# Two weight blocks and one left operand of a down projection loaded on another queue, one of the blocks into its own place

## The chip, the cores and the metric

The kernel runs on one core of a Trainium2 chip. The metric is the device time of one execution in microseconds (us); lower is better. The time before is 1745.2 us, the median of 3 runs (1744.49 to 1745.47). The names of the engines are those of the profile: PE multiplies matrices (PEld are its weight loads), DVE, ACT and POOL work on vectors, and SP issues DMAs. POOL issues DMAs as well, on a queue of its own.

## The reference

One decoder block on 1024 tokens of width 1024, all float32: three gated attention branches, an output projection with a residual, and an MLP. Only the MLP's last line is touched by the change:

```python
h2 = rmsnorm(x, g_mlp_norm[l])
u = jax.nn.relu(jnp.einsum('bsd,df->bsf', h2, w_ff_up[l]))
x = x + jnp.einsum('bsf,fd->bsd', u * u, w_ff_down[l])
```

`w_ff_down` has 4096 rows and 1024 columns. The output is `x`, 1024 by 1024.

## The kernel before

Each float32 operand of a matrix product is split into a rounded part (hi, made by ACT) and the rest (lo, made by DVE as operand minus hi), and a product takes three passes on PE: hi by hi, hi by lo, lo by hi. The large projections are done by a scheme of Strassen's kind: instead of eight block products of a two by two block multiplication there are seven, named P1 to P7, on sums and differences of blocks.

**The up projection** ends in `evict_ops`. Its results, squared and already combined into the seven left operands of the next projection, are stored to a scratch tensor in memory, `s_scr`, by POOL's queue (line 1690), 128 rows of 512 numbers (256 KB) each.

**The down projection** (from `V = Pool("v", ...)` on) runs through `plan`: four groups j of the inner dimension, and in each group the seven products of `DOWN`, in the order P1, P2, P6, P7, P5, P4, P3. Step k of `plan` is one product of one group: four output tiles t, each with 4 blocks by 3 passes, so 48 matmuls of 128x512 (line 2343). While step k runs on PE, the operands of step k+1 are made: `right` makes the weight operand (the sum of blocks on DVE in `right_sum`, then hi on ACT at line 2261, then lo on DVE), `left` makes hi (line 2272) and lo of the left operand. Every two-input operation on DVE goes through the helper `tt`, so all of them carry line 1609.

The weight blocks of a group are w11, w12, w21 and w22, 128 x 2048 numbers (1 MB) each, loaded by `load_wb` (line 2225). They live in four places g0 to g3 of the pool RA by the table `side_of`: w21 in g0, w12 in g1, w22 in g2, w11 in g3. In the first group of the kernel before, w11 is an exception: it goes into the place "t1" of the pool V, and t1 = w12 - w11 is formed in place. The pool V takes over memory that the up projection's tiles have held. The places g0 to g3 hold the operands of P1 and P2 of the up projection until the last such product is done; "g2" and "g3" are those of P2.

The left operands are loaded by `load_s` (line 2233) into three buffers "ur", 1 MB each. The first step's operands are made earlier (`first_load`, `first_split`, line 2162 and after).

Steps in the first group that matter here: k=0 is P1 (operands ready before), k=1 is P2 (w21 as it is, and s of P2), k=2 is P6 (t1 = w12 - w11 and then t2 = w22 - t1, and s of P6), k=3 is P7 (t3 = w22 - w12). In the trace t1 and t2 both read as `t`, the weight operands as `h` (for k=1: `sop`), the hi and lo of the left operands as `sop`, the blocks as `g`, the loaded left operands as `ur`.

The order of work on every engine is the order in which the program is written; nothing reorders it. SP and POOL each issue their DMAs in that order too, and an issue that waits for its place holds everything behind it on the same queue.

Of the kernel before, what the change touches and what calls it, by code (L numbers as in the profile page):

```python
# [21 lines left out]
P = 128  # L22
# [21 lines left out]
def tile_hybrid_block(  # L44
# [20 lines left out]
    nc = tc.nc  # L65
# [58 lines left out]
    s_scr = dram.tile([7 * DFF // 2, S // 2], F32, name="s_scr", tag="s_scr")  # L124
# [1483 lines left out]
    def tt(out_, a_, b_, op):  # L1608
        nc.vector.tensor_tensor(out_, a_, b_, op)  # L1609
# [125 lines left out]
    with tc.manual_schedule():  # L1735
# [79 lines left out]
        rows = [], []  # L1815
# [393 lines left out]
        def vt(tag, dt=F32):  # L2209
            if tag in side_of:  # L2210
                return RA.t(side_of[tag], [P, 4, 512], dt)
            return laid.pop(tag) if tag in laid else V.t(tag, [P, 4, 512], dt)
# [3 lines left out]
        plan = [(j, kind) for j in range(len(groups)) for kind in DOWN]  # L2216
        wb, sraw, sop, top = {}, {}, {}, {}

        def load_wb(j, tag, to=None):
            if j < len(groups):  # L2220
                p, n_ = groups[j]
                wb[j, tag] = vt(to or tag)[:, :n_]
                rows = w_down[2 * p * P:2 * (p + n_) * P, :].rearrange("(c i p) n -> i p c n", i=2, p=P)
                dh = int(tag[2]) - 1
                nc.sync.dma_start(wb[j, tag], rows[int(tag[1]) - 1][:, :, dh * 512:(dh + 1) * 512])

        def load_s(k):
            if k < len(plan):
                j, kind = plan[k]
                p, n_ = groups[j]  # L2230
                sraw[k] = vt("ur")[:, :n_]
                r0 = (DOWN.index(kind) * NP + p) * P
                nc.sync.dma_start(sraw[k], s_scr[r0:r0 + n_ * P, :].rearrange("(c p) n -> p c n", p=P))

        def right_sum(k):

            j, kind = plan[k]
            n_ = groups[j][1]
            if kind == "P6":
                r = wb[j, "t2"] = vt("t2")[:, :n_]  # L2240
                tt(r, wb[j, "w22"], wb[j, "t1"], ALU.subtract)
            elif kind == "P7":
                r = wb[j, "t3"] = vt("t3")[:, :n_]
                tt(r, wb[j, "w22"], wb[j, "w12"], ALU.subtract)
                load_wb(j + 1, "w12")
            elif kind == "P4":
                r = wb[j, "t4"] = vt("t4")[:, :n_]
                tt(r, wb[j, "w21"], wb[j, "t2"], ALU.subtract)
                load_wb(j + 1, "w21")
            else:  # L2250
                r = wb[j, {"P1": "w11", "P2": "w21", "P5": "t1", "P3": "w22"}[kind]]
            return r

        def right(k, part):
            j, kind = plan[k]
            n_ = groups[j][1]
            if part == 0:
                raw = right_sum(k)
                h_, l_ = operand(RA) if k > 1 else (vt("sop", F32R), vt("sop", F32R))
                top[k] = h_[:, :n_], l_[:, :n_], raw  # L2260
                nc.scalar.activation(top[k][0], raw, AF.Copy)  # L2261
            else:
                h_, l_, raw = top[k]
                tt(l_, raw, f32(h_), ALU.subtract)
                if kind == "P3":
                    load_wb(j + 1, "w22")

        def left(k, part):
            n_ = groups[plan[k][0]][1]
            if part == 0:  # L2270
                sop[k] = vt("sop", F32R)[:, :n_], vt("sop", F32R)[:, :n_]
                nc.scalar.activation(sop[k][0], sraw[k], AF.Copy)
            else:
                tt(sop[k][1], sraw[k], f32(sop[k][0]), ALU.subtract)

        sop[0], top[0] = pieces["u"], pieces["w"]
        load_wb(0, "w21")
        for k in (1, 2):
            load_s(k)
        load_wb(0, "w12")  # L2280
        load_wb(0, "w11", "t1")
        load_wb(0, "w22")


        Q = Pool("q", q=2)
# [2 lines left out]
        def late(n):  # L2288
            def rows(kind):
                r0 = (DOWN.index(kind) * NP + place(0)) * P  # L2290
                return s_scr[r0:r0 + P, :]

            def fetch_(key, src):
                q[key] = Q.t("q", [P, 512])
                nc.sync.dma_start(q[key], src)

            def made(kind, key, a_, b_, op):
                tt(q[key], q[a_], q[b_], op)
                keep(kind, 0, q[key])
            if n == 0:  # L2300
                fetch_("a21", u_scr[:, :])
                fetch_("a22", rows("P4"))
            elif n == 1:
                made("P5", "a22", "a21", "a22", ALU.add)
            elif n == 2:
                fetch_("a11", rows("P1"))
            elif n == 3:
                made("P7", "a21", "a11", "a21", ALU.subtract)
            elif n == 4:
                fetch_("s1", rows("P5"))  # L2310
            elif n == 5:
                made("P6", "s1", "s1", "a11", ALU.subtract)
            elif n == 6:
                fetch_("a12", rows("P2"))
            elif n == 7:
                made("P3", "a12", "a12", "s1", ALU.subtract)
# [4 lines left out]
        def out_evict(k, t):  # L2321
            j, kind = plan[k]
            ps = (bx if kind in ("P1", "P6", "P5", "P3") else by)[t]
            s = t if kind in ("P1", "P2", "P3") else 4 + t
            dh = kind in ("P7", "P5", "P3")
            a_ = xr[s][:, dh * 512:(dh + 1) * 512]
            if j == 0 and kind in ("P1", "P6", "P7", "P3"):
                nc.scalar.activation(a_, ps, AF.Copy)
            else:
                tt(a_, a_, ps, ALU.add)  # L2330
            if j == len(groups) - 1 and kind in ("P2", "P5", "P4", "P3"):
                nc.sync.dma_start(out[s * P:(s + 1) * P, dh * 512:(dh + 1) * 512], a_)

        x2t = {}
        for k, (j, kind) in enumerate(plan):
            n_ = groups[j][1]
            for t in range(4):
                ps = (bx if kind in ("P1", "P6", "P5", "P3") else by)[t]
                (sh, sl), (th, tl) = sop[k], top[k][:2]
                qs = slice(t * P, (t + 1) * P)  # L2340
                for c in range(n_):
                    for i, (a_, b_) in enumerate(((sh, th), (sh, tl), (sl, th))):
                        nc.tensor.matmul(ps, a_[:, c, qs], b_[:, c, :],  # L2343
                                         start=(kind in ("P1", "P2", "P7") and c == 0 and i == 0),
                                         stop=(kind in ("P2", "P4", "P3") and c == n_ - 1 and i == 2),
                                         skip_group_check=True)
                if t or k:
                    out_evict(*((k, t - 1) if t else (k - 1, 3)))
                if t == 0 and k:
                    load_s(k + 2)  # L2350
                if k + 1 < len(plan):
                    if t == 0:
                        right(k + 1, 0)
                    elif t == 1:
                        right(k + 1, 1)
                        left(k + 1, 0)
                    elif t == 2:
                        left(k + 1, 1)
                if t == 3 and kind == "P1":
                    wb[j, "t1"] = vt("t1")[:, :n_] if j else wb[j, "w11"]  # L2360
                    tt(wb[j, "t1"], wb[j, "w12"], wb[j, "w11"], ALU.subtract)
                    load_wb(j + 1, "w11")
                if t == 0 and k in (8, 11, 15, 18):
                    x2t[k] = vt("ur").rearrange("p (s c) n -> p s (c n)", s=2)
                    s0 = 2 * (8, 11, 15, 18).index(k)
                    nc.sync.dma_start(x2t[k], x2_scr[s0 * P:(s0 + 2) * P, :].rearrange("(s p) n -> p s n", p=P))
                if t == 3 and k - 1 in x2t:
                    s0 = 2 * (8, 11, 15, 18).index(k - 1)
                    for i in range(2):
                        tt(xr[s0 + i], xr[s0 + i], x2t[k - 1][:, i, :], ALU.add)  # L2370
                if t == 3 and k >= 2:
                    late(k - 2)
# [31 lines left out]
```

## Time and profile before

| | |
|---|---|
| median of 3 runs | 1745.2 us |
| lowest and highest | 1744.49 and 1745.47 us |
| time of the profiled execution | 1743.94 us |
| its span | 1742.2 us |
| first matmul of the down projection | 1421.5 us after the span's start |
| memory read, written | 142.64 MB, 57.15 MB |

The profile is of one execution. The span is the time from the first to the last instruction that the profile shows; the execution's own time is 1.74 us longer. Times in rows of the trace count from the span's start. A row of the timeline gives the start, the duration, the engine, the line, the operation, output and inputs with their shapes, how many instructions of the kind are merged, and in brackets the idle time before and what ended it. The granted TensorE clock is full throughout.

### The profile page before, as it was taken

Reading aid. Unit: us, or ns where it says so; the run is one execution under the profiler, and the core shown is the slowest. Engines: PE = TensorE matmul, PEld = TensorE weight load, DVE = VectorE, ACT = ScalarE, POOL = GpSimd, SP = SyncE. Lnnn points to the kernel's source line nnn. Section 1 sums busy time; section 2 is a strip of 40 time slices with the busy share of each in tenths; the row PEclk is TensorE's granted clock in tenths of the full one; section 3 lists DMA queues with packets and bytes.
Section 4 is the critical chain, followed back from the end, with each engine's and each line's share of the span. In section 5 each row is a group of like instructions: output and inputs, shape, how many; then the busy total and the mean of one; then the engine's idle time right before and its main releaser. Section 6 shows DMA issues by size and latency. Waiting matters only on the chain.

```text
span 1742.2 us, 24834 instructions
## 1 busy us (share of the span) xinstructions
PE 1726.7 (99%) x9426; PEld 1475.3 (85%) x9426; DVE 1262.0 (72%) x2014; ACT 884.8 (51%) x1553; POOL 115.1 (7%) x298
## 2 busy tenths in 40 slices
PE   9999999999999999999999999999999999999999
PEld 9889989888988899899888887878888877888887
DVE  7524578677777567666887699887777776687875
ACT  6525575555566478767974336533332344333331
POOL 0101100000000000010000000121112110000000
PEclk9999999999999999999999999999999999999999
DMA  5241121122132311212354643144344475455531
GB/s 206 73 125 51 50 87 38 42 68 58 36 87 58 90 54 32 78 54 60 117 173 138 225 163 116 43 159 155 133 152 151 145 271 212 156 201 180 194 121 73
DMA packets 136328, 201.41 MB, mean 116 GB/s; under 512 B 9680, under 2 KB 73168, under 8 KB 136208
## 3 DMA queue, kind: packets, MB, share of 16 engines
q1 hardware_dynamic: 127168, 170.20, 30.3%
q0 software_dynamic: 9040, 29.63, 4.9%
q8 instruction: 74, 1.21, 0.3%
q14 instruction: 46, 0.38, 0.1%
HBM read 142.64 MB, written 57.15 MB: 115 GB/s over the span
## 4 chain that ended last, share of the span: by engine, by line
PE 84%; issue 6%; DVE 4%; ACT 2%; POOL 2%; DMA 1%; SPq 0%; POOLq 0%; DVEq 0%; ACTq 0%
PE pp L1040 37%; PE pp L2343 7%; PE pp L1673 6%; PE pv L894 4%; PE tr L2343 4%; PE sc L2343 4%; PE tr L874 4%; PE sc L1673 3%; PE pv L2343 2%; POOL s_scr L1690 1%; PE tr L1673 1%; PE sc L772 1%; PE sc L773 1%; PE tr L1916 1%; PE sc L815 1%
## 5 line engine op out<-in xcount | busy, mean ns | idle before, releaser
L1040 PE MATMUL pp<-hi,whi 128*128 128x512 f32 x496 | 199.1, 401 | 0.0
L1040 PE MATMUL pp<-hi,wlo 128*128 128x512 f32 x496 | 195.8, 395 | 0.0
L1040 PE MATMUL pp<-lo,whi 128*128 128x512 f32 x496 | 195.1, 393 | 0.0
L1040 PE MATMUL pp<-whi,hi 128*128 128x256 f32 (+1 forms) x640 | 183.3, 286 | 0.0
L1040 PE MATMUL pp<-whi,lo 128*128 128x256 f32 (+1 forms) x640 | 179.8, 281 | 0.2 <-DVE lo L487 0.2
L1040 PE MATMUL pp<-wlo,hi 128*128 128x256 f32 (+1 forms) x640 | 179.2, 280 | 0.0
L2343 PE MATMUL pp<-h,sop 128*128 128x512 f32 x540 | 129.0, 395 | 2.3 <-DVE sop L1609 2.3
L881 DVE TENSOR_TENSOR ptl<-tr,pth 128x512 fp32r<-128x512 f32 (+1 forms) x160 | 99.3, 632 | 43.2 <-ACT pth L879 42.3
L2343 PEld LDWEIGHTS pp<-h,sop 128*128 128x128 f32 x540 | 101.1, 187 | 27.7 <-DVE sop L1609 2.6
L879 ACT ACTIVATE pth<-tr 128x512 fp32r<-128x512 f32 (+1 forms) x160 | 86.3, 555 | 70.1 <-PE tr L874 41.8
L1673 PE MATMUL pp<-h,oh 128*128 128x512 f32 x384 | 120.9, 396 | 0.7 <-ACT cu L1759 0.6
L1040 PEld LDWEIGHTS pp<-wlo,hi 128*128 128x128 f32 x640 | 120.5, 188 | 0.9
L1040 PEld LDWEIGHTS pp<-whi,hi 128*128 128x128 f32 x640 | 120.6, 188 | 0.8
L1040 PEld LDWEIGHTS pp<-whi,lo 128*128 128x128 f32 x640 | 120.4, 188 | 0.4 <-DVE lo L487 0.4
L1040 PEld LDWEIGHTS pp<-hi,wlo 128*128 128x128 f32 x496 | 93.1, 188 | 22.9 <-DVE wlo L951 0.3
L951 DVE TENSOR_TENSOR wlo<-raw,whi 128x1024 fp32r<-128x1024 f32 (+1 forms) x72 | 87.7, 1221 | 33.5 <-ACT whi L950 33.1
L1040 PEld LDWEIGHTS pp<-lo,whi 128*128 128x128 f32 x496 | 93.3, 188 | 16.8
L1040 PEld LDWEIGHTS pp<-hi,whi 128*128 128x128 f32 x496 | 93.3, 188 | 16.3
L791 DVE TENSOR_TENSOR_SCAN r<-r,sm 128x896 f32<-128x896 f32 (+3 forms) x64 | 86.2, 1351 | 13.0 <-ACT r L776 12.4
L950 ACT ACTIVATE whi<-raw 128x1024 fp32r<-128x1024 f32 (+1 forms) x72 | 76.2, 1061 | 33.4 <-DMA raw<-w_b 24.7
L1673 PEld LDWEIGHTS pp<-h,oh 128*128 128x128 f32 x384 | 71.7, 187 | 19.2 <-ACT cu L1759 1.5
L2261 ACT ACTIVATE h<-t 128x2048 fp32r<-128x2048 f32 x16 | 30.7, 1921 | 112.3 <-DVE t L1609 99.6
(423 smaller groups left out, 4278.8 us busy)
## 6 DMA issues: line engine op xcount, KB each, us to landing
ur<-s_scr SPq DMA_DIRECT2D x27, 1024.0 KB
raw<-w_in SPq DMA_DIRECT2D x42, 512.0 KB
raw<-w_up SPq DMA_DIRECT2D x60, 256.0 KB
s_scr<-s POOLq DMA_DIRECT2D x60, 256.0 KB, 2.7
g<-w_down SPq DMA_DIRECT2D x15, 1024.0 KB
gate_scr<-o SPq DMA_DIRECT2D x48, 256.0 KB
s_scr<-cu POOLq DMA_DIRECT2D x48, 256.0 KB, 2.9
o<-gate_scr SPq DMA_DIRECT2D x32, 256.0 KB
```

The source lines that it names most:

```text
L772: nc.tensor.matmul(sc[:, :m], q, pair.t["k1", b, ci][:, :m], start=True, stop=False)
L791: nc.vector.tensor_tensor_scan(out=rev, data0=rev, data1=zero.to_broadcast([P, n]), initial=1.0, op0=ALU.mult, op1=ALU.add)
L874: nc.tensor.transpose(tr[:, jj * 256 + a * P:jj * 256 + (a + 1) * P], es[a][:, j * P:(j + 1) * P], ident)
L879: yield Op("ACT", act_time(512 - lo_c), lambda: nc.scalar.activation(ph[:, lo_c:], tr[:, lo_c:], AF.Copy))
L881: yield Op("DVE", dve_time(512 - lo_c), lambda: nc.vector.tensor_tensor(pl[:, lo_c:], tr[:, lo_c:], f32(ph[:, lo_c:]), ALU.subtract))
L894: nc.tensor.matmul(pv[0][:, c_:256], v_of[key][:, j, h4, :], p_[:, jj * 256 + c_:(jj + 1) * 256], start=(k == 0 and n_ == 0 and i == 0), s ...
L950: yield Op("ACT", 0.03 + act_time(m), lambda: nc.scalar.activation(hi, raw, AF.Copy))
L951: yield Op("DVE", dve_time(m), lambda: nc.vector.tensor_tensor(lo, raw, f32(hi), ALU.subtract))
L1040: nc.tensor.matmul(ps, a_, b_, start=(first and i == 0), stop=(last and i == n - 1))
L1673: nc.tensor.matmul(ps, w[a_][:, k * P:(k + 1) * P], h[b_][k], start=(first and k == 0 and i == 0), stop=(last and k == 3 and i == 2), skip ...
L2261: nc.scalar.activation(top[k][0], raw, AF.Copy)
L2343: nc.tensor.matmul(ps, a_[:, c, qs], b_[:, c, :], start=(kind in ("P1", "P2", "P7") and c == 0 and i == 0), stop=(kind in ("P2", "P4", "P3 ...
```

## The change

In the first group, w11 goes to its usual place g3 instead of "t1", and t1 = w12 - w11 is written from g1 and g3 into the place "t1", as in the other groups. The loads of w11, of w22 and of the left operand of k=2 are issued by POOL's queue, in this order, where they stand behind the up projection's stores. SP's queue keeps w21, the left operand of k=1, and w12. The load of the left operand of k=2 stood between those of k=1 and w12; it is now the last of the three on POOL.

```diff
-        def load_wb(j, tag, to=None):
+        def load_wb(j, tag, queue_=nc.sync):
             if j < len(groups):
                 p, n_ = groups[j]
-                wb[j, tag] = vt(to or tag)[:, :n_]
+                wb[j, tag] = vt(tag)[:, :n_]
...
-                nc.sync.dma_start(wb[j, tag], rows[int(tag[1]) - 1][:, :, dh * 512:(dh + 1) * 512])
-
-        def load_s(k):
+                queue_.dma_start(wb[j, tag], rows[int(tag[1]) - 1][:, :, dh * 512:(dh + 1) * 512])
+
+        def load_s(k, queue_=nc.sync):
...
-                nc.sync.dma_start(sraw[k], s_scr[r0:r0 + n_ * P, :].rearrange("(c p) n -> p c n", p=P))
+                queue_.dma_start(sraw[k], s_scr[r0:r0 + n_ * P, :].rearrange("(c p) n -> p c n", p=P))
...
         load_wb(0, "w21")
-        for k in (1, 2):
-            load_s(k)
+        load_s(1)
         load_wb(0, "w12")
-        load_wb(0, "w11", "t1")
-        load_wb(0, "w22")
+        load_wb(0, "w11", nc.gpsimd)
+        load_wb(0, "w22", nc.gpsimd)
+        load_s(2, nc.gpsimd)
...
                 if t == 3 and kind == "P1":
-                    wb[j, "t1"] = vt("t1")[:, :n_] if j else wb[j, "w11"]
+                    wb[j, "t1"] = vt("t1")[:, :n_]
                     tt(wb[j, "t1"], wb[j, "w12"], wb[j, "w11"], ALU.subtract)
                     load_wb(j + 1, "w11")
```

On SP's queue, around the start of the down projection, these are the issues before. The first two are w21 and the left operand of k=1; `ur_13003` is the left operand of k=2, `g_13005` is w12, `t_12999` is w11, `g_13008` is w22, `g_13080` is w11 of the second group, and the last two are the left operands of k=3 and k=4.

```order
L2225 DMA g_13000<-w_down 128x4x512
L2233 DMA ur_12994<-s_scr 128x4x512
L2233 DMA ur_13003<-s_scr 128x4x512
L2225 DMA g_13005<-w_down 128x4x512
L2225 DMA t_12999<-w_down 128x4x512
L2225 DMA g_13008<-w_down 128x4x512
L2225 DMA g_13080<-w_down 128x4x512
L2233 DMA ur_13095<-s_scr 128x4x512
L2233 DMA ur_13158<-s_scr 128x4x512
```

The same stretch of SP's queue with the change:

```order
L2225 DMA g_13000<-w_down 128x4x512
L2233 DMA ur_12994<-s_scr 128x4x512
L2225 DMA g_13003<-w_down 128x4x512
L2225 DMA g_13081<-w_down 128x4x512
L2233 DMA ur_13096<-s_scr 128x4x512
L2233 DMA ur_13159<-s_scr 128x4x512
```

Three loads are gone. The second group's w11 (`g_13081`) now stands right behind w12, and since it goes to the same place g3 as the first group's w11, it has to wait until t1 has been formed.

On POOL's queue, the three loads have come behind the last two stores of the up projection and ahead of a store of the down projection (`q`):

```order
 L1690 DMA s_scr<-cu_12820 128x512
 L1690 DMA s_scr<-s_12973 128x512
-L1690 DMA s_scr<-q_13212 128x512
...
+L2225 DMA g_13005<-w_down 128x4x512
+L2225 DMA g_13007<-w_down 128x4x512
+L2233 DMA ur_13009<-s_scr 128x4x512
+L1690 DMA s_scr<-q_13213 128x512
```

Here `g_13005` is w11, `g_13007` is w22 and `ur_13009` is the left operand of k=2. The numbers of the buffers differ from those before because one more tile is made.

## The prediction

> **What bounds the kernel now.** I read the page first, then the waits of PE from the up projection's end on, then the timelines of DVE, ACT, PE and SP around them.
>
> ```profile
> span 1742.2 us, 24834 instructions
> PE 1726.7 (99%) x9426; PEld 1475.3 (85%) x9426; DVE 1262.0 (72%) x2014; ACT 884.8 (51%) x1553; POOL 115.1 (7%) x298
> ...
> PE pp L2343 <- DVE sop L1609: 2.3, 1, 2.3
> PE sc L2343 <- DVE sop L1609: 0.5, 1, 0.5
> ```
>
> PE is busy for 99% of the span, so only time in which PE stands still can be won. The last two rows are all the waits of PE between 1405 us and the end: one of 2.3 us and one of 0.5 us. They are the ceiling on whatever this change can give. Around them PE, DVE and ACT look like this:
>
> ```profile
> 1438.64 5.60 PE L2343 MATMUL tr<-sop,sop 128*128 128x512 f32 x24
> 1444.08 0.89 PE L2343 MATMUL pp<-h,sop 128*128 128x512 f32 x2
> 1447.26 8.19 PE L2343 MATMUL pp<-h,sop 128*128 128x512 f32 x34 [2.29 <-DVE sop L1609]
> ...
> 1428.97 2.29 DVE L1609 TENSOR_TENSOR sop<-g,sop 128x2048 fp32r<-128x2048 f32 x1 [3.64 <-DMA s_scr<-cu]
> 1431.18 2.29 DVE L1609 TENSOR_TENSOR sop<-ur,sop 128x2048 fp32r<-128x2048 f32 x1
> 1435.16 2.29 DVE L1609 TENSOR_TENSOR t<-g,t 128x2048 f32<-128x2048 f32 x1 [1.69 <-DMA t<-w_down]
> 1437.83 2.29 DVE L1609 TENSOR_TENSOR t<-g,t 128x2048 f32<-128x2048 f32 x1 [0.39 <-DMA g<-w_down]
> 1440.04 0.68 DVE L1609 TENSOR_TENSOR x<-x,sc 128x512 f32<-128x512 f32 x1
> 1442.12 2.29 DVE L1609 TENSOR_TENSOR h<-t,h 128x2048 fp32r<-128x2048 f32 x1 [1.39 <-ACT h L2261]
> 1444.92 2.29 DVE L1609 TENSOR_TENSOR sop<-ur,sop 128x2048 fp32r<-128x2048 f32 x1
> ...
> 1440.16 1.92 ACT L2261 ACTIVATE h<-t 128x2048 fp32r<-128x2048 f32 x1 [6.94 <-DVE t L1609]
> 1441.98 1.91 ACT L2272 ACTIVATE sop<-ur 128x2048 fp32r<-128x2048 f32 x1
> ```
>
> Read it backwards. Step k=2 (P6) begins on PE at 1444.08; its first two matmuls take the hi of the left operand, the third needs its lo. The matmuls follow each other at 5.60/24 = 0.233 us, so the third was due at 1444.08 + 0.47 = 1444.55; it starts at 1447.26, 2.7 us late. The lo is the DVE operation of 1444.92, the last link of a chain on DVE: lo of the weights and of the left operand of k=1 (1428.97 and 1431.18), t1 (1435.16), t2 (1437.83), then hi on ACT (1440.16), lo of the weights (1442.12), an eviction, lo of the left operand. In that chain DVE stands idle twice for a load: 1.69 us for w11 (`t<-w_down`) and 0.39 us for w22 (`g<-w_down`). Its start, 1428.97, hangs on a store of the up projection, whose memory the tile takes over. The small wait of PE, 0.5 us, is for the lo of 1431.18 and hangs on that store too. Why the two loads are late stands in SP's rows:
>
> ```profile
> 1406.65 0.51 SPq L2225 DMA_DIRECT2D g<-w_down  x1
> 1429.73 0.37 SPq L2225 DMA_DIRECT2D t<-w_down  x1
> 1430.20 1.00 SPq L2225 DMA_DIRECT2D g<-w_down  x2
> 1431.26 2.81 SPq L2233 DMA_DIRECT2D ur<-s_scr  x2
> ...
> SPq L2225 <- DMA s_scr<-s: 22.2, 2, 13.5
> ...
> 1410.00:1420.00 10.00, 10.00 (x45) 8.03 (x44) 9.83 (x17) 4.17 (x8) 3.10 (x6) 1.00 1.02 388
> 1426.00:1428.00 2.00, 2.00 (x10) 1.65 (x10) 0.00 (x0) 1.45 (x2) 0.16 (x1) 1.00 0.72 266
> 1428.00:1430.00 2.00, 2.00 (x11) 1.65 (x10) 1.03 (x1) 0.11 (x1) 0.00 (x0) 1.00 0.03 10
> 1432.00:1444.00 12.00, 11.53 (x51) 9.14 (x50) 8.53 (x5) 4.33 (x3) 0.00 (x0) 1.00 1.04 387
> ```
>
> Having issued w12 at 1406.65, SP waits 22.2 us in all for the place t1 to come free of a store, issues w11 at 1429.73, and w22 and the second group's w11 from 1430.20. The windows (last two columns: busy share of the DMA engines, GB/s) show them nearly idle from 1428 to 1430 (10 GB/s) and full from 1432 to 1444 (387 GB/s).
>
> **The change part by part.** *The place.* w11 no longer waits for t1. Its new place g3, like w22's g2, comes free with the last P2 of the up projection, which PE has done by about 1416, three products of 12 x 0.233 = 2.8 us before the down projection begins. So the place costs nothing; what sets the issue is POOL's queue:
>
> ```profile
> 1414.53 1.14 POOL L1690 DMA_DIRECT2D s_scr<-s  x2 [0.19 <-issue]
> 1425.62 0.54 POOL L1690 DMA_DIRECT2D s_scr<-s  x1 [0.19 <-issue]
> ...
> DMA to landing us min/median/max: 2.3/2.8/8.6
> L2162 SPq DMA_DIRECT2D raw<-s_scr x2: 320/320/320, 1402.7 to 1404.7; - x2
> L2225 SPq DMA_DIRECT2D t<-w_down x1: 373/373/373, 1429.7 to 1429.7; - x1
> ```
>
> POOL is through with its last store at 1425.62 + 0.54 = 1426.16, and 0.19 us later can issue w11: 1426.35, against SP's 1429.73.
>
> *The issue of a 1 MB load on POOL* is in no row, since POOL so far only stores 256 KB in 128 rows. Call it g. Bounds: below, 0.54 us as for a store; above, four times that, 2.16 us, if it goes by rows (512 pieces of 2 KB). On SP, 128 rows cost 0.320 us and 512 rows 0.373 us, so there the count hardly matters; by that row I take a value nearer the lower end, 0.6 to 1.2 us.
>
> *From issue to landing.* On SP, w11's issue ended at 1429.73 + 0.37 = 1430.10 and DVE went on at 1435.16: 5.1 us. DVE went on with w22 at 1437.83, 2.7 us later, which is 1.05 MB at 387 GB/s. So on POOL w11 lands at 1426.35 + g + 5.1, and w22 and the left operand of k=2 follow at 2.7 us each: 1432.0, 1434.7, 1437.4 for g = 0.54; 1433.6, 1436.3, 1439.0 for g = 2.16. With a small g the last store's data, 0.26 MB, may still be ahead: at most 0.7 us more (0.26 MB at 387 GB/s).
>
> *What is needed when.* DVE is free for t1 at 1431.18 + 2.21 (two such operations start 2.21 us apart, 1428.97 and 1431.18) = 1433.4. t2 waits for t1: 2.29 + 0.03 later, 1435.7. Hi on ACT then runs from 1438.0 to 1440.0, lo of the weights from 1440.0, and lo of the left operand from 1442.8 to 1445.1, each 2.1 us earlier than before. For that w11 must be there by 1433.4, w22 by 1435.7, and the left operand by 1442.8 - 1.95 = 1440.8 (its hi takes 1.91 us on ACT). For g up to 1435.7 - 2.7 - 5.1 - 1426.35 = 1.55 all are in time. At g = 2.16 w22 is 0.6 us late.
>
> *Sum.* Lo of the left operand at 1445.1 in place of 1447.2: the third matmul of k=2 starts 2.1 us earlier, and 0.6 of the 2.7 us stay, since DVE's own chain from 1428.97 on takes that long. At g = 2.16 the gain is 1.5 us. I take 2.1 us.
>
> *The load of the left operand of k=2* moves from about 1406 to about 1428. The trace before has it waiting long in its buffer; moved, it has some 3 us to spare (1437.4 to 1438.1 against 1440.8). If this cover is gone, each us past 1440.8 costs one, and from 1443.0 on (1444.92 - 1.95) it is worse than before. Its 1 MB leaves the stretch 1410 to 1420, in which the DMA engines are full (388 GB/s); nothing on PE waits there.
>
> *SP's new wait.* The second group's w11 now waits for t1, until 1435.7 instead of 1430.7, and holds the left operands of k=3 and k=4 behind it. By the 5.1 and 2.7 us above they land at about 1443.9 and 1446.6. Are they late?
>
> ```profile
> 1452.94 1.91 ACT L2272 ACTIVATE sop<-ur 128x2048 fp32r<-128x2048 f32 x1
> 1454.88 2.29 DVE L1609 TENSOR_TENSOR sop<-ur,sop 128x2048 fp32r<-128x2048 f32 x1
> 1458.09 2.26 PE L2343 MATMUL sc<-h,sop 128*128 128x512 f32 x9
> ```
>
> The one of k=3 is read at 1452.94 - 2.1 = 1450.8, 7 us after its landing, that of k=4 still later. The lo of k=3 ends at 1457.17 and its third matmul is due at 1458.56; both move by 2.1 us and 1.4 us of slack stays, so PE runs on without another wait. On POOL behind the loads stands only a store of the down projection, tens of us away.
>
> **Rivals.** *Late loads, part of the gain.* POOL's issue takes 1.55 to 3.1 us, or the first data wait behind the stores. For: twice the rows of SP's evidence are missing, POOL's issue has been seen for 128 rows only. At 2.3 us w22 lands 0.75 us late, and the gain is 1.4 us: 1743.8.
>
> *Descriptors on POOL come too slowly: slower than before.* The place is the issue of w22 and of the left operand. w22 lands at 1426.35 + 2g + 0.19 + 5.1 and breaks even at 1437.8, so at g = 3.1 us; at g = 4 it lands at 1439.6 and costs 1.8 us: 1747.0. It could come about if POOL's writing is held while DVE works: DVE is busy without a break from 1428.97 to about 1438.6. Were the third issue held till then, the left operand would land at 1438.6 + 0.6 + 5.1 = 1444.3, 1.3 us past 1443.0: 1746.5. Against it: between 1410 and 1420 DVE is busy for 9.83 of 10 us, and two stores issued at 1414.53 still took 1.14 us together. The Trainium skill ("SBUF — State Buffer", section "Who interferes with whom") has this as a rule: descriptors for a DMA issued from POOL cannot be written while DVE runs in a two-port mode, and the DMA looks blocked; by it such a load belongs on SP. The same section says that a two-input DVE operation of this kind was not seen to stall a DMA, and the row of 1414.53 agrees.
>
> *The store on which DVE's chain starts moves.* It is issued at 1424.90 and gates 1428.97. The loads run at its heels and could hold it up: each us costs one, up to some 1.4 us (the last two stores' 0.52 MB at 387 GB/s), giving 1744.5. Or it lands sooner, because 1 MB of loads has left the full stretch: in the best case both waits of PE go, 2.7 + 0.5 = 3.2 us, 1742.0. Neither is likely: the stores are ahead of the loads on one queue, and from 1426 to 1428 the engines are at 0.72 already before.
>
> *The change does nothing*, because the loads only share one rate: the idle engines of 1428 to 1430 speak against it. 1745.2.
>
> **How the numbers follow.** The profiled execution took 1743.94 us, so the forecast for it is 1741.8 us. It lies 1.26 us under the median of the three runs; against that median, 1745.2, the same 2.1 us give 1743.1 us. Chances: forecast (gain 1.7 to 2.5 us) 0.58; part of the gain, by late loads or a held store, or none, 0.22; a larger gain 0.07; slower than before 0.13, of which 0.08 by over 3.5 us (g of 4.8 us or more). A measurement of this kernel tells from no change about 0.2%, or 3.5 us. All waits of PE in this stretch are 3.2 us, so faster by over 0.2% needs something that no row shows: 0.04. Slower by over 0.2%: 0.08. Within: 0.88. The range goes from the best case, 1742.0, to 1746.4, where the held issue ends; the forecast's own is 1742.6 to 1743.7.
>
> **What will show it.** Right: POOL issues three loads from 1426.4, DVE's waits for `t<-w_down` and `g<-w_down` are gone, t1 starts at 1433.4 and t2 at 1435.7, PE's wait in `pp` shrinks from 2.3 to some 0.3 us, and the 0.5 us in `sc` stay. Wrong: a POOL row over 1.6 us for a load, DVE or ACT waiting for a `g` or `ur` load after 1433, the first lo on DVE starting later than 1429, or a new wait of PE in k=3.

## The result and the profile after

| | before | with the change |
|---|---|---|
| median | 1744.84 us (18 runs) | 1741.53 us (18 runs) |
| lowest and highest | 1743.52 and 1745.62 us | 1741.07 and 1741.96 us |
| profiled execution | 1743.94 us | 1741.96 us |
| ratio of the times, 95% interval | | 0.9982 [0.9975, 0.9989] |

The change is faster by 3.3 us by the medians, or 0.18%. That is 0.5 us past the fast end of the predicted range and 1.2 us more than the 2.1 us of the sum. The two profiled executions differ by 1.98 us only. Both figures are right, and why they differ is what the experiments are about.

First the profile with the change: the page's span and busy rows, all waits of PE from 1400 us to the end (total, times, longest), and PE's timeline where k=1 hands over to k=2 (start, duration, and in brackets the idle time before).

```profile
span 1740.2 us, 24835 instructions
PE 1726.8 (99%) x9426; PEld 1476.1 (85%) x9426; DVE 1261.5 (72%) x2014; ACT 884.1 (51%) x1553; POOL 117.2 (7%) x301
...
PE pp L2343 <- DVE sop L1609: 0.4, 1, 0.4
PE sc L2343 <- DVE sop L1609: 0.2, 1, 0.2
...
1438.60 5.60 PE L2343 MATMUL tr<-sop,sop 128*128 128x512 f32 x24
1444.04 0.63 PE L2343 MATMUL pp<-h,sop 128*128 128x512 f32 x2
1445.10 8.20 PE L2343 MATMUL pp<-h,sop 128*128 128x512 f32 x34 [0.43 <-DVE sop L1609]
```

The third matmul of k=2 starts at 1445.10, before at 1447.26: 2.16 us earlier, and PE's wait there has gone from 2.3 to 0.4 us. PE's busy time is what it was (1726.7 us); only standing still has become less. The rows of DVE and POOL with the change, and the median time from issue to landing of the three loads:

```profile
1428.95 2.29 DVE L1609 TENSOR_TENSOR sop<-g,sop 128x2048 fp32r<-128x2048 f32 x1 [3.35 <-DMA s_scr<-cu]
1431.16 2.28 DVE L1609 TENSOR_TENSOR sop<-ur,sop 128x2048 fp32r<-128x2048 f32 x1
1433.36 2.28 DVE L1609 TENSOR_TENSOR t<-g,g 128x2048 f32<-128x2048 f32 x1
1435.67 2.29 DVE L1609 TENSOR_TENSOR t<-g,t 128x2048 f32<-128x2048 f32 x1
1442.76 2.28 DVE L1609 TENSOR_TENSOR sop<-ur,sop 128x2048 fp32r<-128x2048 f32 x1
...
1426.46 0.76 POOL L2225 DMA_DIRECT2D g<-w_down  x1
1429.50 0.77 POOL L2225 DMA_DIRECT2D g<-w_down  x1 [2.28 <-issue]
1430.27 0.75 POOL L2233 DMA_DIRECT2D ur<-s_scr  x1
...
g<-w_down POOLq DMA_DIRECT2D x2, 1024.0 KB, 6.0
ur<-s_scr POOLq DMA_DIRECT2D x1, 1024.0 KB, 7.8
```

Neither t1 (1433.36) nor t2 (1435.67) has a bracket any more: DVE goes through both without waiting. Taken singly, w11 landed 6.2 us after its issue and w22 5.9 us, at about 1432.7 and 1435.4, so t1 had some 0.7 us to spare and t2 some 0.3.

### The profile page after: what moved, and what is told of

Same layout as the page of the kernel before. It is cut to its first block, busy times and chain, and to the rows that moved or that the text cites. A ratio compares the mean times of both kernels' runs of the same rounds, so it can differ in the third digit from the quotient of the medians.

```text
span 1740.2 us, 24835 instructions
## 1 busy us (share of the span) xinstructions
PE 1726.8 (99%) x9426; PEld 1476.1 (85%) x9426; DVE 1261.5 (72%) x2014; ACT 884.1 (51%) x1553; POOL 117.2 (7%) x301
## 4 chain that ended last, share of the span: by engine, by line
PE 82%; issue 7%; DVE 5%; ACT 2%; POOL 2%; DMA 1%; SPq 0%; POOLq 0%; DVEq 0%; ACTq 0%
PE pp L1040 36%; PE pp L2343 7%; PE pp L1673 6%; PE pv L894 4%; PE tr L2343 4%; PE sc L2343 4%; PE tr L874 3%; PE sc L1673 3%; PE pv L2343 2%; POOL s_scr L1690 1%; PE tr L1673 1%; PE tr L1916 1%; PE sc L772 1%; PE sc L815 1%; PE sc L773 1%
```

## The experiments

Each is against the kernel before, timed beside it on one chip; the kernel before had a median of 1744.99, 1745.0 and 1745.08 us in the three sets (labels e, f and g), each of which ran on another chip. Diffs are against the changed kernel unless it is said otherwise.

**The kernel before again, with a profile of its own.** No edit. The open question was where the other 1.2 us come from: longer waits at this place in the executions of the median, or time gained elsewhere.

> The kernel before, unchanged, for a second profile. The change gave 3.3 us between the medians, 2.0 between the two profiles, 2.1 by the forecast's sum. Theory A: the profiled execution before was one with short waits; in most executions w11 and w22 land up to 1.2 us later, and the change takes this spread away too. Then a profile of an execution near 1745 us shows PE waiting about 3.5 us in all at the start of k=2 (2.7 in the first profile), DVE waiting 2 to 3 us for the two loads (2.1 in the first). Theory B: the extra 1.2 us lies elsewhere. Then the waits are 2.7 and 2.1 us as before, and the down projection starts about 1 us later than 1421.5. An execution near 1743.9 us decides nothing. Median 1744.8 by both.

1744.58 us (1743.27 to 1746.71, 11 runs), ratio 0.9999 [0.999, 1.0008]. Its profiled execution took 1744.95 us and is one of those in the middle of the median's runs, 1.0 us longer than the first. The same stretch of PE's timeline and windows of it (stretch, length, busy time of PE, PEld, DVE, ACT and POOL, then the granted TensorE clock, DMA share, GB/s):

```profile
1443.43 1.03 PE L2343 MATMUL pp<-h,sop 128*128 128x512 f32 x2
1446.76 9.72 PE L2343 MATMUL pp<-h,sop 128*128 128x512 f32 x34 [2.29 <-DVE sop L1609]
...
1444.00:1448.00 4.00, 1.71 (x6) 1.19 (x7) 4.00 (x5) 0.00 (x0) 0.00 (x0) 1.00 0.06 24
1448.00:1452.00 4.00, 4.00 (x12) 3.16 (x11) 2.10 (x1) 1.87 (x2) 0.00 (x0) 0.57 0.21 27
```

The first profile of the kernel before, in the same window:

```profile
1448.00:1452.00 4.00, 4.00 (x18) 3.20 (x18) 2.61 (x2) 1.36 (x1) 0.00 (x0) 1.00 0.21 14
```

The wait is no longer (2.29 us, as in the first profile), and the down projection began at 1421.15, not later than the 1421.53 of the first. The difference lies behind the wait: the clock falls to 0.57 in the mean of these 4 us (0.50 for most of it), 12 matmuls fall into it instead of 18, and the same 34 matmuls take 9.72 us instead of 8.19. That is 1.53 us, lost to nothing that waits. In windows of 20 us over PE's work from start to end, only the one around this place is below 1.00 in that execution, and in the first profile none is. So neither theory of the first set stood, and a third was formed, theory C: a wait of this length lets the clock fall behind it, in most executions but not in the one that was profiled first.

**The place alone**: w11 into g3, all loads on SP in the order of the kernel before.

```diff
         load_s(1)
+        load_s(2)
         load_wb(0, "w12")
-        load_wb(0, "w11", nc.gpsimd)
-        load_wb(0, "w22", nc.gpsimd)
-        load_s(2, nc.gpsimd)
+        load_wb(0, "w11")
+        load_wb(0, "w22")
```

> w11 in its own place g3, and all loads on SP in the order of before (w21, s1, s2, w12, w11, w22). If it is the place that counts, SP issues w11 right behind w12 at about 1407 us or when P2 of the up projection is done (1416), both blocks land before 1430, DVE waits for neither, and the time is that of the change, 1741 to 1742.5. If POOL's queue counts, 1744.8. A third way: 2 MB more in the stretch 1410 to 1422, whose DMA engines are full, hold up the stores; then the first lo on DVE starts after 1429 and each us of that costs one.

1745.69 us (1745.13 to 1746.69, 11 runs), ratio 1.0005 [0.9996, 1.0014]: the whole gain is gone. SP's, the windows', DVE's and PE's rows:

```profile
1406.18 10.34 SPq L2225 DMA_DIRECT2D g<-w_down  x3
...
1420.00:1426.00 6.00, 6.00 (x28) 4.95 (x27) 4.73 (x8) 2.88 (x3) 3.24 (x6) 1.00 1.04 407
1426.00:1430.00 4.00, 4.00 (x19) 3.30 (x19) 0.00 (x0) 1.56 (x3) 0.00 (x0) 1.00 1.04 409
1434.00:1438.00 4.00, 2.26 (x5) 1.48 (x6) 4.00 (x3) 0.00 (x0) 0.00 (x0) 0.54 0.00 0
...
1431.99 2.29 DVE L1609 TENSOR_TENSOR sop<-g,sop 128x2048 fp32r<-128x2048 f32 x1 [7.12 <-DMA s_scr<-cu]
1436.40 2.28 DVE L1609 TENSOR_TENSOR t<-g,g 128x2048 f32<-128x2048 f32 x1
...
PE sc L2343 <- DVE sop L1609: 3.4, 2, 2.0
```

SP issues w12, w11 and w22 from 1406.18 to 1416.5, ten microseconds earlier than POOL. They are there in time (t1 has no bracket), but they keep the DMA engines full (407 and 409 GB/s) exactly while the last stores must land. DVE's chain hangs on such a store and waits 7.12 us for it, against 3.35 with the change. The chain begins 3 us late, PE waits 3.4 us, and the clock falls after that. The Trainium skill ("DMA: Bandwidth & Descriptors", section "Issuing engines are not separate DMA queues") says that DMAs of all issuing engines share the same 16 DMA engines and interleave; the trace agrees in that loads on SP's queue hold up a store on POOL's.

**The queue alone**: against the kernel before, three loads on POOL as in the change, but w11 still in "t1".

```diff
...
-        for k in (1, 2):
-            load_s(k)
+        load_s(1)
         load_wb(0, "w12")
-        load_wb(0, "w11", "t1")
-        load_wb(0, "w22")
+        load_wb(0, "w11", nc.gpsimd, "t1")
+        load_wb(0, "w22", nc.gpsimd)
+        load_s(2, nc.gpsimd)
```

> w11 in the old place t1, but w11, w22 and the left operand of k=2 on POOL behind the stores. If the place counts, POOL waits for t1 until about 1429.5 and issues w11 as late as SP did, w11 lands at 1435.3, w22 at 1438, the left operand at 1441: PE waits as before or 0.5 us longer, 1744.8 to 1745.5. If the queue counts, 1741.5.

1752.38 us (1751.39 to 1753.88, 5 runs), ratio 1.0045 [1.0032, 1.0057]: 7 us slower, far worse than had been expected. The timelines of SP, POOL and DVE:

```profile
1415.18 0.37 SPq L2225 DMA_DIRECT2D g<-w_down  x1
...
1432.81 0.76 POOL L2225 DMA_DIRECT2D t<-w_down  x1 [7.36 <-ACT x L2328]
...
1431.43 2.29 DVE L1609 TENSOR_TENSOR sop<-g,sop 128x2048 fp32r<-128x2048 f32 x1 [6.81 <-DMA s_scr<-cu]
1438.86 2.29 DVE L1609 TENSOR_TENSOR t<-g,t 128x2048 f32<-128x2048 f32 x1 [2.94 <-DMA t<-w_down]
1444.29 2.29 DVE L1609 TENSOR_TENSOR t<-g,t 128x2048 f32<-128x2048 f32 x1 [3.13 <-DMA g<-w_down]
```

POOL has to wait for "t1" just as SP did, and three loads stand in line there. What made it so costly is what SP now does: nothing on its queue waits for t1, so the second group's w11 goes out at 1415.18 (with the change 1435.71) and k=3's left operand behind it. They meet the stores as in the experiment before (6.81 us), so the place comes free still later, w11 and w22 are late by 2.94 and 3.13 us, PE waits for 6.7 us in four waits, and the clock falls twice (0.60 in the mean from 1434 to 1438, 0.66 from 1450 to 1460). So the two parts are worth the gain only together, and a part that the prediction called harmless, SP's wait for t1, is what keeps the DMA engines clear for the stores.

**The left operand of k=2 back on SP**, between those of k=1 and w12.

```diff
         load_s(1)
+        load_s(2)
...
-        load_s(2, nc.gpsimd)
```

> The change, but the left operand of k=2 back on SP between s of k=1 and w12. If its 1 MB in the full stretch 1410 to 1420 holds up the last cu store, the first lo on DVE comes 0.3 us later after the store's issue (4.07 us as before, 3.79 with the change), and the time is 0.3 us above the change, 1741.8. If it does not, 1741.5 and a landing as with the change. By theory A of the first run, the spread of the runs is under 1 us as with the change, since w11 and w22 still come early.

1741.25 us (1741.04 to 1744.52, 11 runs of which 10 lie below 1742), ratio 0.9982 [0.9973, 0.9991]. PE's waits are the 0.4 and 0.2 us of the change. Moving that load to POOL gains nothing.

**Work put into the wait**: against the kernel before, ten more matmuls where PE waits, into a bank that is overwritten later. They add work, and the output does not depend on them.

```diff
+                        if k == 2 and t == 0 and c == 0 and i == 1:
+                            for _ in range(10):
+                                nc.tensor.matmul(by[0], sop[1][0][:, 0, qs], top[1][0][:, 0, :], start=True, stop=True,
+                                                 skip_group_check=True)
```

> The kernel before, with 10 extra matmuls on PE in the wait of k=2, between its second and third matmul, into a bank whose content is overwritten afterwards; they take 10 x 0.233 = 2.3 of the 2.7 us in which PE would stand idle. Theory C (found in the second profile of before): the wait lets the granted clock fall to 0.5 for about 3.3 us in most executions, which costs 1.5 us on top of the wait, and in the others nothing. Then the extra work makes the kernel faster: no stretch below 1.00 behind the wait, runs within 1 us of each other, median 1743.6, 1.2 us under before. Rival D: the spread of the runs comes from elsewhere; then the median is 1744.8 as before with the same spread of 2 us, or above it by what of the extra work doesn't fit.

1743.53 us (1742.78 to 1744.08, 11 runs), ratio 0.9991 [0.9982, 1.0]; the kernel before took 1745.0 us beside it. PE's timeline and the window behind the wait:

```profile
1444.93 2.44 PE L2349 MATMUL sc<-sop,sop 128*128 128x512 f32 x10
1447.39 8.20 PE L2343 MATMUL pp<-h,sop 128*128 128x512 f32 x34
...
1448.00:1452.00 4.00, 4.00 (x19) 3.22 (x18) 2.74 (x2) 1.23 (x1) 0.00 (x0) 1.00 0.03 7
```

DVE's chain is as late as before, the 34 matmuls begin no earlier, and yet the kernel is 1.5 us faster, because they run at full clock (8.20 us). It is theory C by itself: the fall of the clock is gone, though the third matmul starts no earlier. The interval just reaches no change; the clock speaks more plainly: 10 of the 11 executions record a mean of 1.000, of the kernel before 15 of 82 (the table further down).

**Half of that work**: five more matmuls in place of ten, so that PE stands still for half the time.

> The kernel before with 5 in place of 10 extra matmuls in the wait of k=2: PE stands idle for about 1.2 us instead of 2.3. The order of DVE and the loads are as before, so the third matmul of k=2 starts when it did. By theory C in its sharp form, where the whole idle time must be long enough, the clock stays at 1.00 and the median is 1743.6, as with 10. If half the idle time trips it too, the median lies between 1743.6 and 1744.9, with some runs near each.

1743.55 us (1742.97 to 1744.96, 11 runs), ratio 0.9995 [0.9986, 1.0004], beside 1745.08 us. The interval takes in no change, so the size is less sure than the profile:

```profile
1446.29 8.20 PE L2343 MATMUL pp<-h,sop 128*128 128x512 f32 x34 [1.16 <-DVE sop L1609]
...
1448.00:1452.00 4.00, 4.00 (x19) 3.19 (x18) 2.01 (x2) 2.34 (x3) 0.00 (x0) 1.00 0.27 65
```

1.16 us of standing still leave the clock at 1.00 here. One of the 11 executions records 0.999 and took 1744.96 us, so the fall may not be quite gone.

**The left operand of k=2 first on POOL**, ahead of w11 and w22.

```diff
+        load_s(2, nc.gpsimd)
         load_wb(0, "w11", nc.gpsimd)
         load_wb(0, "w22", nc.gpsimd)
-        load_s(2, nc.gpsimd)
```

> The change with the order on POOL turned round: left operand of k=2 first, then w11, then w22. It doses the lateness of the two blocks. POOL issues them at about 1426.4, 1429.5 and 1430.3, they land at 1432.7, 1435.4 and 1438.1; t1 starts at 1435.4 and t2 at 1438.1 in place of 1433.4 and 1435.7, so PE waits about 2.4 us more than with the change, as long as before. By the sum alone 1741.5 + 2.4 = 1743.9. By theory C the clock falls in most executions too: 1744.5 to 1745.5, with a spread of up to 2 us. If the gap of 2.3 us on POOL behind the first load belongs to w11 itself and not to the first place, w22 lands 2 us later still, 1746.

1746.46 us (1743.82 to 1747.88, 11 runs), ratio 1.0007 [0.9999, 1.0016]: slower than expected. POOL's and PE's timelines and the window:

```profile
1425.44 0.76 POOL L2233 DMA_DIRECT2D ur<-s_scr  x1
1428.50 1.51 POOL L2225 DMA_DIRECT2D g<-w_down  x2 [2.30 <-issue]
...
1447.71 10.48 PE L2343 MATMUL pp<-h,sop 128*128 128x512 f32 x33 [2.30 <-DVE sop L1609]
...
1448.00:1452.00 4.00, 4.00 (x10) 3.13 (x10) 3.05 (x3) 0.91 (x1) 0.00 (x0) 0.50 0.04 16
```

The gap of 2.3 us on POOL stands again behind the first of the three loads, though this is another load; the two behind it are issued back to back. PE waits 1.2 us and then 2.30 us, and the clock stays at 0.50 through the whole window. The row counts 33 of the 34 matmuls; all 34 took 10.71 us, against 9.72 us behind the one wait of the kernel before. In windows of half a us the clock is at 0.50 for some 6.8 us here, and for some 3.4 us there; it is some 6.8 us as well in the place alone and in the layout that follows, where two waits also lie close together.

**Another layout, to free DVE's first operation from the store.** The tile that DVE writes at 1428.95 was to lie in memory that comes free earlier.

```diff
-                for tag in ("ur", "sop", "t4", "t3", "t2", "t1")}
+                for tag in ('sop', 'ur', 't4', 't3', 't2', 't1')}
```

> The change, with the tiles of the down projection laid out in another order (sop first), so that the lo operands of k=1 no longer take over the memory of the last stored cu tile. Should the store's landing be what holds DVE's chain at 1429, the chain now starts at 1425.6, the wait in sc (0.3 us) is gone, and t1 and t2 hang on the landing of the loads alone (1432.7 and 1435.4, 0.7 and 0.3 us earlier than with the change): 0.3 to 0.6 us under the change, 1740.9 to 1741.2. If not, 1741.5.

1748.86 us (1748.06 to 1749.62, 11 runs), ratio 1.0022 [1.0012, 1.0031]. The timelines of DVE and SP:

```profile
1425.37 2.28 DVE L1609 TENSOR_TENSOR sop<-g,sop 128x2048 fp32r<-128x2048 f32 x1
1438.10 2.29 DVE L1609 TENSOR_TENSOR t<-g,g 128x2048 f32<-128x2048 f32 x1 [5.29 <-DMA g<-w_down]
...
1421.85 0.37 SPq L2233 DMA_DIRECT2D ur<-s_scr  x1
```

The wait for the store went, as meant (1425.37, no bracket), but `ur` has taken over the late memory: its load goes out at 1421.85 instead of 1405.94, w12 stands behind it on SP's queue, and t1 starts at 1438.10. The stall moved to the queue. The same layout with w11 on SP too went the same way:

> As the run before, and w11 from SP behind w12 (issued at about 1415.5 when its place is free), w22 and the left operand of k=2 from POOL. With the store's landing off DVE's chain, 1 MB more in the full stretch should cost nothing; w22, now the first on POOL, lands at 1432.7, t1 starts by 1430.2 to 1432 and t2 by 1434.3, and PE waits for nothing: 0.9 us under the change, 1740.6. If the stores are held up so that t1's place, which waits for the last of them, comes free after 1433, 1741.5 or more.

1750.44 us (1749.86 to 1751.71, 6 runs), ratio 1.0031 [1.002, 1.0043]; t1 starts at 1440.33, and PE waits 5.0 and 2.0 us.

**The left operand's lo ahead of an eviction**: the left operand of k=2 on SP as above, and its lo, the last link of the chain, one place earlier on DVE.

```diff
+                if (k, t) == (1, 2):
+                    left(2, 1)
                 if t or k:
                     out_evict(*((k, t - 1) if t else (k - 1, 3)))
...
-                    elif t == 2:
+                    elif t == 2 and k != 1:
                         left(k + 1, 1)
```

> The change, with the left operand of k=2 on SP as in the fourth run, and DVE's lo of that operand moved ahead of the eviction of sc's second tile in k=1 (0.6 us). The lo then ends 0.6 us earlier against PE, the rest of the wait in pp (0.43 us) goes, the wait in sc (0.2 us) stays: 0.4 us under the change, 1740.8 to 1741.1. If the eviction moved back holds up PE in k=3, or the rest of the wait hangs on something else, 1741.3 or more.

1740.64 us (1740.44 to 1742.62, 11 runs), ratio 0.9979 [0.997, 0.9988]: the lowest median, 0.6 us below the 1741.25 of the version that it is built on, though that one ran in another set and the two intervals overlap. The waits of PE (all that is left) and the timelines of DVE and PE:

```profile
PE sc L2343 <- DVE sop L1609: 0.2, 1, 0.2
...
1441.52 2.29 DVE L1609 TENSOR_TENSOR sop<-ur,sop 128x2048 fp32r<-128x2048 f32 x1
1443.40 8.66 PE L2343 MATMUL pp<-h,sop 128*128 128x512 f32 x36
```

All 36 matmuls of k=2 run in one row, without a wait.

**The change again**, beside these.

> The change itself once more, on the same chip as the run before. By theory C its PE waits (0.2 and 0.4 us) never trip the clock: no stretch below 1.00 at the start of the down projection, runs within 1 us of each other, median 1741.5. By rival D the runs spread over 2 us in this set too.

1741.72 us (1741.07 to 1744.76, 11 runs), ratio 0.9985 [0.9977, 0.9994]. Four of the 11 lie above 1742, where none of the first 18 did; the narrow spread that was expected did not hold. The profiled execution is one of the four, 1743.2 us. Its timelines of DVE and PE and its loads:

```profile
1434.32 2.29 DVE L1609 TENSOR_TENSOR t<-g,g 128x2048 f32<-128x2048 f32 x1 [1.71 <-DMA g<-w_down]
...
g<-w_down POOLq DMA_DIRECT2D x2, 1024.0 KB, 8.2
```

The blocks took 8.2 us to land in the median instead of 6.0; with some 0.7 and 0.3 us to spare, DVE waits 1.71 us for w11, PE waits 2.3 us in `pp` as in the kernel before, and nearly all of the gain is gone in that execution. (The clock did not fall in this one.) One suspect is the third load, which shares the DMA engines with the two blocks, but nothing shows it: with the left operand of k=2 on SP, 2 of 22 runs lie above 1742, with the change 4 of 29 over both sets.

## Why the prediction was right in its steps and wrong in its size

*What bounds the kernel: right as far as waits go.* PE waited for DVE's chain, and the chain for w11 and w22. With both there in time the chain ran through.

*POOL's issue: right within its bounds.* 0.76 us for a load of 1 MB, where 0.54 to 2.16 was allowed and 0.6 to 1.2 taken. That the loads follow at 2.7 us each because they share one rate was not what set w22: POOL issued it 3.04 us behind w11 (0.76 + 2.28 of a gap that no row of before could show). By chance this is nearly the same spacing.

*The place costs nothing: right.* The last P2 begins three products before the down projection, 8.4 us, and ends two before it, at about 1416; the prediction's "three products" is off by one, and nothing hangs on it.

*The deadlines: right.* t1 at 1433.4 and t2 at 1435.7 were forecast; 1433.36 and 1435.67 were measured. The lo of the left operand ends at 1445.04 (forecast 1445.1).

*The sum of the waits: right.* The third matmul of k=2 starts 2.16 us earlier (forecast 2.1). It was due at 1444.04 + 0.47 = 1444.51 and is 0.59 us late (forecast 0.6). The 0.5 us in `sc` became 0.2 only because the down projection began at 1421.79 in this execution, 0.26 us later than in the first profile of before, while DVE's first lo began at the same time. The profiled execution took 1741.96 us (forecast 1741.8).

*The move of the left operand costs nothing: right* (1741.25 with it back on SP). *SP's new wait: right* that nothing is late behind it, but its other side was missed: it holds 2 MB of loads out of the stretch in which the stores land.

*The rival of late loads: seen in one execution, not in the median.* It took most of the gain in the profiled execution of the repeat. POOL's issue took 0.76 us there too, so the slow issue that the rival named first was not the reason; whether the data waited is open.

*Where it failed.* The step is "It lies 1.26 us under the median of the three runs; against that median, 1745.2, the same 2.1 us give 1743.1 us." It took the distance between the profiled execution and the median for an offset that the change leaves alone. It was part of the price of the very wait that the change removes. The profiled execution of before was one of a minority in which the clock did not fall, and the sentence that the clock is full throughout was true of such executions only. The premise, "so only time in which PE stands still can be won", failed with it: behind the wait PE was busy for 9.72 us with what takes 8.19 us at full clock, and that time could be won too. The mean granted clock that each execution records, rounded to a thousandth (1.7 us of a run), shows it over the 82 executions of the kernel before beside the experiments:

| mean clock | executions | median time | lowest and highest |
|---|---|---|---|
| 1.000 | 15 | 1743.4 us | 1742.94 and 1744.13 us |
| 0.999 | 58 | 1745.1 us | 1743.0 and 1746.02 us |
| 0.998 | 9 | 1746.4 us | 1745.22 and 1747.12 us |

With work in the wait, ten and five matmuls, 10 of 11 executions each record 1.000. With the change 15 of 18 do, and the three at 0.999 are no slower (1741.29 to 1741.71 us), so one rounded figure alone decides nothing; the two windows of the kernel before and the two fills do. The sum that should have stood is 2.1 us of wait and 1.5 us of clock behind it in most executions: from 1745.2 to about 1741.6. Against the 1744.84 us of the 18 runs it gives 1741.2, 0.3 us less than was measured; this rest stays open.

The same step shifted the range: its fast end, 1742.0, was the removal of all waits (3.2 us) from the median, as if nothing but waiting could be won. For the profiled execution the forecast was right; had the number been left there, it would have lain within the change's runs. (At the slow end the working of the held issue gives 1746.5, not 1746.4.)

## What to carry to other kernels

A wait of PE can cost its own length and the clock behind it: here 2.3 us of waiting cost another 1.5 us in most executions, so before a wait is priced, look at the granted clock in the windows behind it, in more than one execution. When the profiled execution is not the median, find what the others have that it lacks before its distance is carried along as a constant. An issue that stands blocked on a queue may be what keeps transfers apart: whoever unblocks it should ask what lands in the stretch that fills up.

## What the runs showed of the hardware that was not expected

- **The clock fell behind waits of about 2 us.** In the second profile of the kernel before it came down to 0.50 for some 3.4 us behind a wait of 2.29 us; in the first profile and in that of the change's repeat, with waits as long (2.29 and 2.30 us), not at all. It fell behind 2.0 us (the place alone) and behind 1.69 us with a second wait close behind (the queue alone); in the five profiles whose waits are 1.2 us or shorter it did not. The Trainium skill ("TensorE: Matmul & The Clock Gate", "Part 1: The HAM clock gate") has the clock halve after at least one idle window of about 3.4 us and says that the window runs freely. The trace agrees on the half clock, and the stretch at 0.50 is about one such window long, but waits well under 3.4 us were enough, and the measurement decides. That executions with the same wait differ would fit a window that runs freely; no run here shows it.
- **A gap of 2.3 us on POOL behind the first of the large loads**, 2.27 to 2.30 us in the seven profiles in which the next load's place was free, whichever load it is and whether two or three are issued; where the third load's place was free too, it was issued right behind the second. What fills the gap stays open.
- **Loads on another queue hold up a store of 256 KB**: DVE waited for it 3.35 us with the change and 7.12 us with w12, w11 and w22 issued ahead of it.
- **1 MB took 6.0 us to land from POOL in one profile and 8.2 us in another** of the same kernel; why was not settled.
